# One hand-written issue order for the opening of layer 0, and four smaller moves

## The chip, the cores and the metric

The kernel runs on one core of one Trainium2 chip. The metric is the time of one execution on the device in microseconds (us), as the median of several runs. The core has five engines with a queue each: PE multiplies matrices (its weight loads are listed as PEld), DVE does vector work, ACT evaluates functions, POOL is a second, general engine for vector work, and SP issues the DMA transfers here. Each engine works through its own list of instructions in order, and semaphores make one wait for another.

## The reference

Two layers work on 512 latent tokens and 256 context tokens of width 1024. Cut to what the change touches:

```python
sc, scc = silu(c), silu(c_ctx)                  # the two conditions
for l in range(2):
    shift, scale, gate = split(sc @ w_mod[l] + b_mod[l])        # context: the same with scc
    hx = rms_norm(x, norm_w[l]) * (1 + scale) + shift           # hc: context, with its own shift and scale
    z  = hx @ w_in[l]                           # q, k, v of three attentions, LRU, gates, merges
    # three attentions (MLA, windowed SWA, dense AXA) and an RG-LRU, each times silu(gate),
    # projected and summed with sigmoid(merge) weights
    x  = x + gate * (mix @ w_out[l])            # context too, in layer 0 alone
# the RG-LRU uses softplus(-lambda), the same numbers for all tokens
```

## The kernel before, in words

Activations lie with channels on the 128 partitions. The width of 1024 is eight tiles `xk[k]`, each with 512 columns of latent and 256 of context. Products that need more than one pass of reduced precision are split: a number is a high part (fp32r, made by ACT) and a low part (the rest, made by a subtraction), and `mm3` (lines 193 to 197) multiplies high by high, low by high and high by low. So each weight slot passes DMA, ACT (`hi`) and POOL (`lo`, line 190) before PE can finish with it, and each `hx` tile passes ACT twice (lines 331, 332) and DVE once (line 333).

The opening of layer 0 (lines 893 to 970) does these things:

- `cond` (line 252, PE, and 254, ACT) spreads the two condition vectors over all partitions as rows `crow` in the buffer `P`. It is done three times: in the opening, again in the LRU stage of layer 0 and again late in layer 1, since `P` is used by attention in between.
- `sumsq`, `rstd_cols`, `rstd_rows` find 1/rms of each token: squares on ACT, sums over tiles on DVE (line 290), over partitions on PE (line 299), the power on POOL (line 304), and PE spreads it to `rb` in PSUM (line 310). `normal` (line 929) multiplies `xk` with it on DVE, for latent and context.
- `scale_pe` (line 227) makes the scales of two tiles on PE from 1 MB of `wmod0`, followed by two transposes (line 232) and two small DVE steps (lines 236, 238). `shift0` (line 243) makes the shift of one tile and one stream on DVE from a 128x1024 product; there are 16 of these.
- `hx_split` makes the high and low parts of `hx`, and `first` multiplies them with the weights of `sq` and `skv`, the projections of SWA, into six PSUM tiles `tk`: tiles t = 0 and 2 are latent, t = 4 is context.

After the opening come the head norms of these six products (`head_norm`, lines 384 to 410, with several steps on POOL each), the product of `akv` (`tg`, lines 195 to 197), two gates (`fg`), and then attention with projections beside it. `vectors` (lines 148 to 176) makes softplus by a chain of small DVE steps and a power on POOL.

The order in which instructions stand on each engine is set by the framework's scheduler, which plays the program through with its own estimates; `issue_after` binds one instruction behind another. The weights of the opening share a ring of two raw buffers (line 187) with all others.

Of the kernel before, what the change touches and what calls it, by code (L numbers as in the profile page):

```python
# [6 lines left out]
F32 = mybir.dt.float32  # L7
# [52 lines left out]
NS = len(SLOT)  # L60


def body(tc, xT, ccol, wmod, wmod0, pvec, rvec, tabs, wall, out):
# [5 lines left out]
    with st:  # L69
# [64 lines left out]
        xs = dp.tile([4, 128, 2, SEQ], F32, name="xs")  # L134

# [6 lines left out]
        def consts():  # L142
            sp.dma_start(out=tb, in_=tabs[:, :TB_N])
            mask = raw_take()[:, :256]
            sp.dma_start(out=mask, in_=tabs[:, TB_N:])
            dve.tensor_copy(out=maskb, in_=mask)

        def vectors():
# [72 lines left out]
        def scale_pe(c, scol, ws, p, pm):  # L221
# [9 lines left out]
            for e in range(2):  # L231
                last = pe.matmul(out=pm[:, 2 * e:2 * e + 2], lhsT=r[0:2, e * 128:e * 128 + 128], rhs=ident[0:2, 0:2],
                          start=True, stop=True, skip_group_check=True)
# [6 lines left out]
            return last  # L240
# [41 lines left out]
        def sumsq(xk, k, state, acc=None):  # L282
# [43 lines left out]
        def hx_split(k, i, h, xk):  # L326
# [6 lines left out]
            dve.tensor_tensor(out=h[:, 1, sl], in0=xk[:, sl], in1=h[:, 0, sl].bitcast(F32), op=ALU.subtract)  # L333
# [175 lines left out]
        pend = []  # L509

# [37 lines left out]
        def attn_tail(P, L, den, t0, nl, v, vh, done):  # L548
            dve.reciprocal(out=den, in_=den)
# [341 lines left out]

        scol = silu_col()
        xt = [big(f"x{kp}") for kp in range(4)]
        for kp in range(4):
            sp.dma_start(out=xt[kp][:, :, :SEQ], in_=xT[kp][:, :, :SEQ])
        wm = [mod0_load(0)]
        sp.dma_start(out=pv, in_=pvec)
        for kp in range(4):
            sp.dma_start(out=xt[kp][:, :, SEQ:], in_=xT[kp][:, :, SEQ:])
        xk = [xt[k // 2][:, k % 2, :] for k in range(KT)]  # L900
        sc = [cond(scol, i, crow[i]) for i in range(2)]
        states = [{}, {}]
# [4 lines left out]
        bank = lambda name: ps.tile([128, 512], F32, name=name, tag=name)  # L907
        rb, mp = bank("rb"), bank("mp")
        w0 = {'sq': [], 'skv': []}
# [3 lines left out]
        def wload0(key):  # L913
            hi, lo = [sb.tile([128, 512], F32R, name="w0", tag="w0", bufs=16) for i in range(2)]
            return wsplit(0, key, 512, hi, lo)

        def first(k, ts):
# [9 lines left out]
        def normal(i, k):  # L927
            o, n = SEGS[i]
            dve.tensor_tensor(out=xk[k][:, o:o + n], in0=xk[k][:, o:o + n], in1=rb[:, :n], op=ALU.mult)
# [5 lines left out]
        ms = rstd_cols(states[0], SEQ, mp[:, 384:])  # L935
        last = [scale_pe(0, scol, wm[0], mp, mp[:, 256:])]
        rstd_rows(ms, SEQ, rb)
        for c in range(4):
            for g in w0:
                w0[g].append(wload0((g, c)))  # L940
            if c < 3:
                wm.append(mod0_load(c + 1))
                with tc.issue_after(last[0].ins):
                    last[0] = scale_pe(c + 1, scol, wm[c + 1], mp, mp[:, 256:])
            ks = (2 * c, 2 * c + 1)
            for k in ks:
                shift(0, k)
            if c == 0:
                for k in range(KT):
                    normal(0, k)  # L950
            for k in ks:
                hx_split(k, 0, hx[k], xk[k])
                shift(1, k)
            for k in ks:
                first(k, (0, 2))
            if c == 0:
                for k in range(KT):
                    sumsq(xk[k][:, SEQ:], k, states[1], rawt[:, 1024:1280])
                with tc.issue_after(last[0].ins):
                    ms = rstd_cols(states[1], CTX, mp[:, 384:])  # L960
# [233 lines left out]
```

## Time and profile before

| | |
|---|---|
| median of 3 runs | 1438.25 us (1431.86 to 1442.55) |
| the profiled execution | 1437.18 us, of it 1435.1 us from its first to its last instruction |
| PE busy | 1357.7 us, 95% of the span |
| DVE, ACT, POOL busy | 895.2, 675.9 and 712.3 us |
| chain that ended last | PE 72%, DVE 9%, POOL 7%, DMA 5%, issue 4%, ACT 3% |
| mean granted clock of TensorE | 0.98 of full speed |

The opening is the first 90 us of the 1435. The page gives its busy time in slices of 36 us, which is too coarse, so the rows below are from views with smaller windows. In the view of stretches each row is a stretch of time; then comes its length, the busy time and instruction count of PE, PEld, DVE, ACT and POOL, the granted TensorE clock (1 is the full 2.4 GHz, 0.5 is 1.2 GHz), the DMA engines' busy share and GB/s. In the timeline each row gives the start, the busy time, the engine, the line of the kernel, the operation, what it writes and reads with shapes, and how many are merged; brackets hold the idle time before it and what ended it.

### The profile page before, as it was taken

The numbers are of one execution on the slowest core, as the hardware profiler recorded it, in microseconds if no ns is written. First come the engines' busy times: TensorE is split into PE (matmuls) and PEld (weight loads), VectorE is DVE, ScalarE is ACT, GpSimd is POOL, SyncE is SP. The second block draws the span as 40 slices with busy tenths as digits, with TensorE's granted clock in tenths as the row PEclk, the third lists the DMA queues.
The fourth block names the chain that finished last, engine by engine and source line by source line (L and its number), as shares of the span: only waits on it lengthen the run. The fifth ranks groups of instructions, "written<-read, shape, count | busy, mean of one in ns | idle before, by whom it ended". The sixth has DMA issues, their size and how long they took to land.

```text
span 1435.1 us, 21997 instructions
## 1 busy us (share of the span) xinstructions
PE 1357.7 (95%) x8216; PEld 1189.2 (83%) x8216; DVE 895.2 (62%) x1473; ACT 675.9 (47%) x1413; POOL 712.3 (50%) x691
## 2 busy tenths in 40 slices
PE   6898999999999999999999889999999999898998
PEld 4697989999998897888888778998887777776786
DVE  7756876456747656677445777876577576466441
ACT  4544555445544444562232344655555454465331
POOL 1453614223624625577553466455345563478663
PEclk8899999999999999999999999999999999999999
DMA  9301101111111212322335732112221111222544
GB/s 353 92 5 59 34 16 55 42 45 39 54 37 38 59 30 81 103 65 98 125 114 158 234 95 75 45 48 74 67 61 45 61 57 39 59 67 66 188 153 144
DMA packets 58746, 117.81 MB, mean 82 GB/s; under 512 B 6544, under 2 KB 10640, under 8 KB 58640
## 3 DMA queue, kind: packets, MB, share of 16 engines
q1 hardware_dynamic: 58640, 116.42, 25.7%
q8 instruction: 64, 1.05, 0.3%
q14 instruction: 42, 0.34, 0.1%
HBM read 112.20 MB, written 4.19 MB: 81 GB/s over the span
## 4 chain that ended last, share of the span: by engine, by line
PE 72%; DVE 9%; POOL 7%; DMA 5%; issue 4%; ACT 3%; SPq 0%; POOLq 0%; ACTq 0%; DVEq 0%
PE fg L196 9%; PE fg L195 9%; PE fg L197 9%; PE pvo L567 4%; DMA wraw<-in_wall_dram 3%; PE tg L197 3%; PE tg L196 3%; PE tg L195 3%; PE s L587 3%; POOL wlo L190 3%; PE pj L195 2%; PE pj L196 2%; PE pj L197 2%; PE ptr L560 2%; PE ptr L561 2%
## 5 line engine op out<-in xcount | busy, mean ns | idle before, releaser
L190 POOL TENSOR_TENSOR wlo<-wraw,whi 128x512 fp32r<-128x512 f32 (+2 forms) x290 | 398.8, 1378 | 360.9 <-ACT whi L189 347.3
L196 PE MATMUL fg<-hx,wlo 128*128 128x512 f32 (+1 forms) x864 | 314.2, 364 | 12.3 <-POOL wlo L190 12.3
L195 PE MATMUL fg<-hx,whi 128*128 128x512 f32 (+1 forms) x864 | 313.9, 365 | 7.9 <-ACT whi L189 5.0
L197 PE MATMUL fg<-hx,whi 128*128 128x512 f32 (+1 forms) x864 | 312.0, 361 | 0.0
L189 ACT ACTIVATE whi<-wraw 128x512 fp32r<-128x512 f32 (+2 forms) x290 | 179.8, 621 | 229.2 <-DMA wraw<-in_wall_dram 154.4
L196 PEld LDWEIGHTS fg<-hx,wlo 128*128 128x128 f32 x864 | 166.4, 193 | 38.9 <-POOL wlo L190 16.3
L195 PEld LDWEIGHTS fg<-hx,whi 128*128 128x128 f32 x864 | 165.6, 192 | 33.8 <-ACT whi L189 7.1
L197 PEld LDWEIGHTS fg<-hx,whi 128*128 128x128 f32 x864 | 166.1, 192 | 22.2
L564 DVE TENSOR_TENSOR PT<-ptr,PT 128x512 fp32r<-128x512 f32 (+1 forms) x148 | 98.5, 672 | 60.6 <-ACT PT L563 59.3
L196 PE MATMUL tg<-whi,hx 128*128 128x256 f32 (+1 forms) x432 | 122.5, 285 | 1.9 <-DVE hx L323 1.9
L195 PE MATMUL tg<-whi,hx 128*128 128x256 f32 (+1 forms) x432 | 122.2, 285 | 1.8 <-ACT hx L322 1.2
L197 PE MATMUL tg<-wlo,hx 128*128 128x256 f32 (+1 forms) x432 | 121.5, 284 | 1.4 <-POOL wlo L190 1.4
L563 ACT ACTIVATE PT<-ptr 128x512 fp32r<-128x512 f32 (+1 forms) x148 | 84.7, 585 | 79.6 <-PE ptr L561 70.0
L537 ACT ACTIVATE P<-s,nm 128x768 f32<-128x768 f32 (+3 forms) x120 | 91.9, 771 | 55.7 <-DVE nm L532 30.1
L530 DVE TENSOR_REDUCE nm<-s 128x2 f32<-128x1536 f32 (+3 forms) x60 | 86.0, 1434 | 29.5 <-PE s L197 16.9
L865 POOL TENSOR_TENSOR acc<-acc,gt 128x768 f32<-128x768 f32 (+1 forms) x48 | 81.1, 1690 | 24.1 <-DVE gt L861 23.2
L196 PEld LDWEIGHTS tg<-whi,hx 128*128 128x128 f32 x432 | 82.6, 191 | 2.8 <-DVE hx L323 2.5
L195 PEld LDWEIGHTS tg<-whi,hx 128*128 128x128 f32 x432 | 82.5, 191 | 2.8 <-ACT hx L322 1.4
L197 PEld LDWEIGHTS tg<-wlo,hx 128*128 128x128 f32 x432 | 82.4, 191 | 2.2 <-POOL wlo L190 2.0
L853 ACT ACTIVATE gt<-fg 128x512 f32<-128x512 f32 x84 | 44.1, 525 | 74.5 <-PE fg L197 70.9
L551 DVE TENSOR_SCALAR P<-P,den 128x768 f32<-128x768 f32 (+3 forms) x120 | 77.4, 685 | 1.8
L560 PE MATMUL ptr<-ident,P 128*128 128x128 f32 x288 | 72.9, 279 | 1.9 <-DVE gt L861 1.8
(302 smaller groups left out, 3137.2 us busy)
## 6 DMA issues: line engine op xcount, KB each, us to landing
wraw<-in_wall_dram SPq DMA_DIRECT2D x286, 256.0 KB, 2.6
raw<-in_wmod_dram SPq DMA_DIRECT2D x32, 512.0 KB, 3.6
wmp<-in_wmod_dram SPq DMA_DIRECT2D x16, 512.0 KB, 8.6
x<-in_xT_dram SPq DMA_DIRECT2D x4, 512.0 KB, 5.7
xs<-xn SPq DMA_DIRECT2D x4, 512.0 KB, 3.9
gt<-xs SPq DMA_DIRECT2D x8, 256.0 KB, 2.9
out_dram<-xn SPq DMA_DIRECT2D x4, 512.0 KB, 3.8
wraw<-in_wall_dram SPq DMA_DIRECT2D x8, 160.0 KB, 2.2
```

Of the source, the lines that this page charges most:

```text
L189: act.activation(out=hi[:, :n], in_=raw, func=AF.Copy)
L190: pool.tensor_tensor(out=lo[:, :n], in0=raw, in1=hi[:, :n].bitcast(F32), op=ALU.subtract)
L195: pe.matmul(out=o, lhsT=a[0], rhs=b[0], start=first, stop=False, skip_group_check=True)
L196: pe.matmul(out=o, lhsT=a[1], rhs=b[0], start=False, stop=False, skip_group_check=True)
L197: pe.matmul(out=o, lhsT=a[0], rhs=b[1], start=False, stop=last, skip_group_check=True)
L530: dve.tensor_reduce(out=nm, in_=s3, axis=AX.X, op=ALU.max, negate=True)
L537: act.activation(out=P[i][:, :L], in_=s3[:, i, :], func=AF.Exp, scale=scale, bias=nm[:, i:i + 1], accum_out=den[:, i:i + 1])
L551: dve.tensor_scalar(out=P[i][:, :L], in0=P[i][:, :L], scalar1=den[:, i:i + 1], scalar2=None, op0=ALU.mult)
L560: pe.transpose(tr[:, e * 256:e * 256 + 128], P[0][:, ca:ca + 128], ident)
L563: act.activation(out=q[:, :n], in_=tr[:, :n], func=AF.Copy)
L564: dve.tensor_tensor(out=q[:, 512:512 + n], in0=tr[:, :n], in1=q[:, :n].bitcast(F32), op=ALU.subtract)
L865: pool.tensor_tensor(out=a[:, :N], in0=a[:, :N], in1=t[:, :N], op=ALU.add)
```

## The change

A wrapper `InOrder` binds every instruction that goes through it behind the one before it on its engine. The opening is written out in full with all five engines wrapped, so its order no longer comes from the scheduler. The new order is one list: which product comes when is written by hand, context's products of tiles 0 and 1 stand ahead of the latent products of tiles 4 and 5, and the load of `akv` (with its two subtractions per pair on POOL) closes the list. Besides:

- Two times 20 products of a bf16 identity with itself stand on PE before and after the opening's `cond`.
- For context, the sums of squares (line 290 before), the multiplication with 1/rms (line 929 before) and the low part of `hx` (line 333 before) go from DVE to POOL; the row of 1/rms is first copied from PSUM to SBUF by ACT (`rbc`), and POOL reads that.
- The eight weights of the opening have a ring of four raw buffers of their own.
- `vectors` runs later: its DVE steps are chained behind a reciprocal of an attention, where before they lay from 16 us on.
- The condition rows are written to DRAM (`cs`) once and read back by DMA in layers 0 and 1 where `cond` was repeated.

```diff
+class InOrder:
+    def __init__(self, tc, eng, last=None):
+        self.tc, self.eng, self.last = tc, eng, last
+    def __getattr__(self, name):
+        f = getattr(self.eng, name)
+        def call(*a, **k):
+            if self.last is None:
+                self.last = f(*a, **k)
+            else:
+                with self.tc.issue_after(self.last.ins):
+                    self.last = f(*a, **k)
+            return self.last
+        return call
...
-        def vectors():
+        def vectors(last):
+            dve = InOrder(tc, nc.vector, last)
...
-                dve.tensor_tensor(out=state['acc'][:, :n], in0=state['acc'][:, :n], in1=sq[:, :n], op=ALU.add)
+                eng = pool if acc is not None else dve
+                eng.tensor_tensor(out=state['acc'][:, :n], in0=state['acc'][:, :n], in1=sq[:, :n], op=ALU.add)
...
-            dve.tensor_tensor(out=h[:, 1, sl], in0=xk[:, sl], in1=h[:, 0, sl].bitcast(F32), op=ALU.subtract)
+            (pool if i else dve).tensor_tensor(out=h[:, 1, sl], in0=xk[:, sl], in1=h[:, 0, sl].bitcast(F32), op=ALU.subtract)
...
+        pe, act, dve, pool, sp = (InOrder(tc, e) for e in (nc.tensor, nc.scalar, nc.vector, nc.gpsimd, nc.sync))
...
+        def warm(n):
+            for i in range(n):
+                pe.matmul(out=mp[:, 384:512], lhsT=identb, rhs=identb, start=True, stop=True, skip_group_check=True)
...
+        warm(20)
         sc = [cond(scol, i, crow[i]) for i in range(2)]
+        warm(20)
...
+        rstd_rows(ms, CTX, rb)
+        act.activation(out=rbc, in_=rb[:, :CTX], func=AF.Copy)
+        for k in range(KT):
+            pool.tensor_tensor(out=xk[k][:, SEQ:], in0=xk[k][:, SEQ:], in1=rbc, op=ALU.mult)
+        w0_split(r0[2])
+        first(2)
+        turn()
+        scale_add(2, col(2))
+        first(3)
+        for k in (4, 5):
+            shift(0, k)
+        for k in (4, 5):
+            latent(k)
+        for k in (2, 3):
+            shift(1, k)
+        turn = scale_pe(3, scol, wm[3], mp, col(3))
+        for k in (0, 1):
+            context(k)
+        w0_split(r0[3])
+        for k in (0, 1):
+            first(k, (4,))
+        turn()
+        scale_add(3, col(3))
+        for k in (4, 5):
+            first(k)
...
+        akv = tload(0, 'akv')
+        boot = dve.last
+        pe, act, dve, pool, sp = nc.tensor, nc.scalar, nc.vector, nc.gpsimd, nc.sync
         consts()
+        for i in range(2):
+            sp.dma_start(out=cs[i], in_=sc[i])
...
             if l == 0:
-                with tc.issue_after(wdma[0].ins):
-                    vectors()
+                vectors(mark[0])
...
             if l == 0:
-                sc = [cond(scol, i, crow[i]) for i in range(2)]
+                for i in range(2):
+                    sp.dma_start(out=sc[i], in_=cs[i])
...
             if l == 1:
-                sc = [cond(scol, 0, crow[0])]
+                sp.dma_start(out=sc[0], in_=cs[0])
```

How the change moves instructions is shown at three places. In these rows `w_` are weights, with an even and odd number for high and low parts, `xms` is 1/rms, `wmp_0` to `wmp_3` the four 512 KB pieces of a group of modulation weights, and a line of "..." stands for rows left out. In the new program nearly all rows have the line of the wrapper, 76.

POOL in the opening, before:

```order
L304 TENSOR_TENSOR xms<-xms,mhalf 128x4
L190 TENSOR_TENSOR w_216<-wraw,w_215 128x512
L190 TENSOR_TENSOR w_222<-wraw,w_221 128x512
L190 TENSOR_TENSOR w_337<-wraw,w_336 128x512
L190 TENSOR_TENSOR w_343<-wraw,w_342 128x512
L190 TENSOR_TENSOR w_460<-wraw,w_459 128x512
L304 TENSOR_TENSOR xms<-xms,mhalf 128x2
```

POOL in the opening, now:

```order
L76 TENSOR_TENSOR raw<-raw,gt 128x256 x7
L76 TENSOR_TENSOR w_381<-w0r,w_380 128x512
L76 TENSOR_TENSOR w_385<-w0r,w_384 128x512
L76 TENSOR_TENSOR xms<-xms,mhalf 128x2
L76 TENSOR_TENSOR x_118<-x_118,raw 128x256 x2
L76 TENSOR_TENSOR x_119<-x_119,raw 128x256 x2
L76 TENSOR_TENSOR x_120<-x_120,raw 128x256 x2
L76 TENSOR_TENSOR x_121<-x_121,raw 128x256 x2
L76 TENSOR_TENSOR w_440<-w0r,w_439 128x512
L76 TENSOR_TENSOR w_444<-w0r,w_443 128x512
L76 TENSOR_TENSOR hx_0_242<-x_118,hx_0_242 128x256
L76 TENSOR_TENSOR hx_1_243<-x_118,hx_1_243 128x256
```

Seven sums, eight multiplications and eight low parts of context (six of these come later) now stand between the subtractions of the weights.

PE around the last group of scales, before (`tk_189` and `tk_190` are the two products of context):

```order
L232 MATMUL mp<-ident,raw 128x2 x2
L195 MATMUL tk_189<-w_215,hx_0_175 128x256
L195 MATMUL tk_190<-w_221,hx_0_175 128x256
L227 MATMUL mp<-wmp_0_471,scol 2x256 x4
L227 MATMUL mp<-wmp_1_472,scol 2x256 x4
L196 MATMUL tk_189<-w_215,hx_0_175 128x256
```

PE at the same place, now (`tk_254` and `tk_255` are the products of context):

```order
L76 MATMUL mp<-wmp_0_407,scol 2x256 x4
L76 MATMUL mp<-wmp_1_408,scol 2x256 x4
L76 MATMUL tk_254<-w_276,hx_0_242 128x256 x2
L76 MATMUL tk_254<-w_277,hx_0_242 128x256
...
L76 MATMUL mp<-ident,raw 128x2 x2
L76 MATMUL tk<-w_439,hx_4_246 128x256 x2
```

Between the two parts of the last piece stand the rest of context's products of tiles 0 and 1; the latent products of tiles 4 and 5 stand behind them.

SP's transfers up to the second group of scale weights, before:

```order
L218 DMA wmp_2_125<-in_wmod_dram 128x1024
L897 DMA consts<-in_pvec_dram 128x114
L218 DMA wmp_3_126<-in_wmod_dram 128x1024
L899 DMA x_115<-in_xT_dram 128x2x256
L899 DMA x_116<-in_xT_dram 128x2x256
L216 DMA wmp_0_227<-in_wmod_dram 128x1024
L188 DMA wraw<-in_wall_dram 128x512
L216 DMA wmp_1_228<-in_wmod_dram 128x1024
L218 DMA wmp_2_229<-in_wmod_dram 128x1024
L188 DMA wraw<-in_wall_dram 128x512
```

SP's transfers up to the same weights, now:

```order
L76 DMA wmp_3_129<-in_wmod_dram 128x1024
L76 DMA consts<-in_pvec_dram 128x114
L76 DMA w0r<-in_wall_dram 128x512 x2
L76 DMA x_118<-in_xT_dram 128x2x256
L76 DMA x_119<-in_xT_dram 128x2x256
L76 DMA x_120<-in_xT_dram 128x2x256
L76 DMA x_121<-in_xT_dram 128x2x256
L76 DMA wmp_0_143<-in_wmod_dram 128x1024
L76 DMA wmp_1_144<-in_wmod_dram 128x1024
```

All of context and the first two weights now stand ahead of the second group of scale weights.

## Rows read from the trace of the kernel before

**Rows 1.** The page's first line: length of the profiled execution

```profile
span 1435.1 us, 21997 instructions
```

**Rows 2.** Stretches: length, busy PE, PEld, DVE, ACT, POOL, clock, DMA share, GB/s

```profile
0.00:15.00 15.00, 8.56 (x40) 8.31 (x40) 5.40 (x13) 8.11 (x15) 0.68 (x6) 0.93 0.82 288
15.00:31.10 16.10, 12.56 (x44) 4.84 (x44) 15.96 (x34) 5.95 (x13) 5.11 (x3) 0.75 1.04 398
31.10:65.00 33.90, 26.61 (x148) 18.78 (x147) 29.44 (x73) 16.83 (x29) 14.17 (x10) 0.85 0.40 135
65.00:88.70 23.70, 23.70 (x195) 23.40 (x195) 8.85 (x19) 11.62 (x24) 5.44 (x6) 1.00 0.13 34
88.70:106.30 17.60, 17.60 (x148) 17.46 (x146) 14.42 (x35) 6.68 (x20) 16.50 (x21) 1.00 0.01 2
106.30:124.10 17.80, 12.60 (x72) 10.21 (x71) 12.33 (x23) 7.72 (x20) 12.58 (x14) 0.94 0.28 86
...
200.00:250.00 50.00, 50.00 (x368) 46.89 (x368) 32.95 (x69) 28.52 (x77) 17.06 (x28) 1.00 0.14 43
```

**Rows 3.** Timeline of PE: start, busy time, engine, line, operation, idle before

```profile
3.31 6.69 PE L252 MATMUL scb<-ident,scol 128*128 128x128 f32 x32 [3.31 <-DVE scol L209]
...
25.90 5.30 PE L227 MATMUL mp<-wmp,scol 128*2 128x256 f32 x16 [3.29 <-DVE mod L236]
...
31.80 0.60 PE L232 MATMUL mp<-ident,raw 2*128 2x2 f32 x4
...
50.20 3.62 PE L227 MATMUL mp<-wmp,scol 128*2 128x256 f32 x16
...
108.02 0.50 PE L196 MATMUL fg<-hx,wlo 128*128 128x512 f32 x1 [1.55 <-POOL wlo L190]
```

**Rows 4.** Timeline of ACT in the opening and at its end

```profile
22.74 0.63 ACT L189 ACTIVATE w<-wraw 128x512 fp32r<-128x512 f32 x1 [1.33 <-DMA wraw<-in_wall_dram]
...
83.96 0.60 ACT L491 ACTIVATE raw<-tk 128x512 f32<-128x512 f32 x1 [5.11 <-PE tk L197]
```

**Rows 5.** Timeline of POOL where DVE works beside it

```profile
20.20 1.77 POOL L190 TENSOR_TENSOR w<-wraw,w 128x512 fp32r<-128x512 f32 x1 [2.85 <-ACT w L189]
23.45 1.27 POOL L190 TENSOR_TENSOR w<-wraw,w 128x512 fp32r<-128x512 f32 x1 [1.47 <-ACT w L189]
42.41 4.00 POOL L190 TENSOR_TENSOR w<-wraw,w 128x512 fp32r<-128x512 f32 x2 [17.69 <-ACT w L189]
```

**Rows 6.** Timeline of DVE at the same times, and a step of softplus

```profile
20.77 2.01 DVE L290 TENSOR_TENSOR raw<-raw,gt 128x256 f32<-128x256 f32 x2
22.70 3.07 DVE L929 TENSOR_TENSOR x<-x,rb 128x512 f32<-128x512 f32 x5
...
41.77 1.28 DVE L243 CUSTOM_DVE_ANT_0 raw<-wmp,P,consts 128x1024 bf16<-128x1024 f32 x1
...
42.97 2.30 DVE L243 CUSTOM_DVE_ANT_0 wmp<-wmp,P,consts 128x1024 f32<-128x1024 f32 x1
...
45.21 1.75 DVE L333 TENSOR_TENSOR hx<-x,hx 128x512 fp32r<-128x512 f32 x1
...
54.69 0.17 DVE L163 TENSOR_TENSOR sp_ab<-sp_ab,sp_u 128x8 f32<-128x8 f32 x1
```

**Rows 7.** Timeline of POOL: small powers, the head norms' begin, a gate's weight

```profile
49.47 0.70 POOL L304 TENSOR_TENSOR xms<-xms,mhalf 128x2 f32<-128x2 f32 x1
50.14 1.63 POOL L156 TENSOR_TENSOR sp_u<-ebase,sp_ab 128x8 f32<-128x8 f32 x1
...
86.03 0.57 POOL L373 TENSOR_SCALAR hn_ss<-hn_ss 128x8 f32<-128x8 f32 x1 [16.05 <-DVE hn_ss L393]
...
106.65 1.32 POOL L190 TENSOR_TENSOR wlo<-wraw,whi 128x512 fp32r<-128x512 f32 x1
```

**Rows 8.** Timeline of POOL in the MLA stage: a step with 256 columns

```profile
539.85 0.73 POOL L682 TENSOR_TENSOR y<-y,pvt 64x256 f32<-64x256 f32 x1 [2.65 <-DVE pvt L681]
```

**Rows 9.** Chain of waits, layers 0 and 1: start (us), duration (us), what

```profile
544.26 0.89 PE scb L252 x8
...
1327.14 2.70 DMA wraw<-in_wall_dram
```

More of the change, by code (lines that the diff above doesn't have):

```diff
@@ L230, in scale_pe, with scale_add @@
             act.activation(out=r[0:2, :256], in_=p[0:2, :256], func=AF.Copy)
-            for e in range(2):
-                last = pe.matmul(out=pm[:, 2 * e:2 * e + 2], lhsT=r[0:2, e * 128:e * 128 + 128], rhs=ident[0:2, 0:2],
-                          start=True, stop=True, skip_group_check=True)
+            return lambda: [pe.matmul(out=pm[:, 2 * e:2 * e + 2], lhsT=r[0:2, e * 128:e * 128 + 128], rhs=ident[0:2, 0:2],
+                                      start=True, stop=True, skip_group_check=True) for e in range(2)]
+        def scale_add(c, pm):
             f = 8 + 2 * c
@@ L509, in body @@
         pend = []
+        mark = [None]
         def attn_flush():
@@ L548, in attn_tail @@
         def attn_tail(P, L, den, t0, nl, v, vh, done):
-            dve.reciprocal(out=den, in_=den)
+            mark[0] = dve.reciprocal(out=den, in_=den)
             for i in range(2):
@@ L933, in shift @@
             shift0(k, i, sc[i], w, w if i else rawt[:, 1536:2048].bitcast(BF16))
-        ms = rstd_cols(states[0], SEQ, mp[:, 384:])
-        last = [scale_pe(0, scol, wm[0], mp, mp[:, 256:])]
-        rstd_rows(ms, SEQ, rb)
[L938 to L960, printed above, removed]
-                last[0] = states[1]['ins']
-                rstd_rows(ms, CTX, rb)
-            for k in ks if c else ():
-                normal(1, k - 2)
-                hx_split(k - 2, 1, hx[k - 2], xk[k - 2])
-                first(k - 2, (4,))
@@ L967, in body, with latent, context @@
-        for k in (6, 7):
-            normal(1, k)
-            hx_split(k, 1, hx[k], xk[k])
-            first(k, (4,))
+        def latent(k):
+            hx_split(k, 0, hx[k], xk[k])
+        rbc = rawt[:, 1280:1536]
+        def context(k):
+            hx_split(k, 1, hx[k], xk[k])
+        col = lambda c: mp[:, 260 + 4 * c:264 + 4 * c]
+        turn = scale_pe(0, scol, wm[0], mp, col(0))
+        ms = rstd_cols(states[0], SEQ, mp[:, 288:])
+        turn()
+        scale_add(0, col(0))
+        w0_split(r0[0])
@@ new lines, in body @@
+        for k in (0, 1):
+            shift(0, k)
+        rstd_rows(ms, SEQ, rb)
+        for k in (0, 1):
+            normal(k)
+        for k in (0, 1):
+            latent(k)
+        turn = scale_pe(1, scol, wm[1], mp, col(1))
+        for k in range(2, KT):
+            normal(k)
+        first(0)
+        turn()
+        scale_add(1, col(1))
+        first(1)
+        for k in range(KT):
+            sumsq(xk[k][:, SEQ:], k, states[1], rawt[:, 1024:1280])
+        w0_split(r0[1])
+        r0.append(w0_load(2))
@@ new lines, in body @@
+        ms = rstd_cols(states[1], CTX, mp[:, 288:])
+        for k in (2, 3):
+            shift(0, k)
+        for k in (2, 3):
+            latent(k)
+        for k in (0, 1):
+            shift(1, k)
+        wm.append(mod0_load(3))
+        r0.append(w0_load(3))
+        turn = scale_pe(2, scol, wm[2], mp, col(2))
+        rstd_rows(ms, CTX, rb)
+        act.activation(out=rbc, in_=rb[:, :CTX], func=AF.Copy)
+        for k in range(KT):
+            pool.tensor_tensor(out=xk[k][:, SEQ:], in0=xk[k][:, SEQ:], in1=rbc, op=ALU.mult)
@@ new lines, in body @@
+        for k in (6, 7):
+            shift(0, k)
+        for k in (6, 7):
+            latent(k)
+        for k in (2, 3):
+            context(k)
+            first(k, (4,))
+        for k in (6, 7):
+            first(k)
+        for k in (4, 5, 6, 7):
+            shift(1, k)
+        for k in (4, 5, 6, 7):
+            context(k)
+            first(k, (4,))
+        akv = tload(0, 'akv')
+        boot = dve.last
+        pe, act, dve, pool, sp = nc.tensor, nc.scalar, nc.vector, nc.gpsimd, nc.sync
```

50 lines of the change are left out of this document (36 added, 14 removed).

## The prediction

> **What bounds the kernel now.** The kernel as a whole is bound by PE. But the opening, where the change lies, is bound by something else in each stretch, so I read the view of stretches first [rows 2]. From 0 to 15 us the data arrive; from 15 to 31.1 DVE is busy 15.96 of 16.1 us while PE has 12.56 at a granted clock of 0.75; from 31.1 to 65 PE works 26.61 of 33.9 and DVE 29.44; from 65 on PE works without a gap. So about 3.5 + 7.3 = 10.8 us of PE idle time lie between 15 and 65, and only they can be won, together with the clock. The end of this stage is not PE alone: the products `tk` end at 88.7, and POOL starts on the head norms at 86.03, 16.05 us after its last work [rows 7], 2.1 us after ACT emptied the first `tk` at 83.96 [rows 4]. From there POOL is busy 16.50 of 17.6 us [rows 2], and the gate's `wlo` comes at 106.65 at the end of POOL's chain [rows 7]; PE waited 1.55 us for it and goes on at 108.02 [rows 3]. What the opening gives is therefore what POOL's start moves, as long as PE's own `akv` is not later.
>
> The timeline of PE says what an idle time costs twice: 3.29 us of idle before 25.90, and then the scales of two tiles in 5.30 us, which take 3.62 at 50.20 [rows 3]. The timelines of POOL and DVE side by side [rows 5, 6] show a second matter. A subtraction of 128x512 on POOL takes 1.27 us at 23.45, though DVE multiplies with PSUM beside it in its usual 3.07/5 = 0.61. But at 20.20 it takes 1.77, while two DVE additions of SBUF with SBUF take 2.01; at 42.41 two take 4.00, while DVE's shift takes 2.30 for 1.28 and its subtraction 1.75. Steps that read two SBUF operands on both engines go one after the other here.
>
> This rests on rows alone. The Trainium skill, page "SBUF — State Buffer", section "Who interferes with whom", says the same: the ports that the two engines share are an exclusive lock, which a DVE step with two SBUF inputs contends for with a POOL step that reads SBUF, and a DVE step with one such input does not; the rows agree. It speaks against moving work to POOL here. Against it stands its page "Perfetto Trace Analysis", section "Optimizing Scalar/DVE Operations", by which moving work from a saturated vector engine may make sense, with a warning of that port: by the first, all 23 moved steps cost DVE time; by the second they cost none and the first rival's time results.
>
> **The new opening, worked as a list.** Prices from rows: a matmul of `tk` 23.70/195 = 0.12 us [rows 2], so 24 for a latent tile 2.9 and 12 for a context tile 1.45; scales 3.6, two transposes and any spread 0.6 [rows 3]; POOL 1.3 for 128x512, 0.70 for a small power [rows 7], and 0.73 for 256 columns (the nearest row has 64 partitions, [rows 8]; between 0.6, half of 1.27, and 1.0); DVE 1.28 for a shift and 0.6 for a subtraction [rows 5, 6].
>
> The 40 added products of the identity stand where PE has nothing else: the first twenty before `scol` (PE waited 3.31 us for it, [rows 3]), the others between `cond`'s end at 10.0 and the first weights. At the 0.12 us of a `tk` product twenty take 2.4 us; cost 0, at most 1 us if the weights come early.
>
> *Start.* The second piece of the second group of scale weights now has as many bytes ahead of it as the second `wraw` had, which ACT got at 22.74 [rows 4]. So PE begins those scales at 22.7 (25.90 before) and ends at 26.3; latent tile 0, transposes, latent tile 1: 32.7. Context's squares stand on ACT behind the copy of those scales, so POOL's seven sums run from 27.4 for 5.1 us, to 32.5: level with PE. Then 0.5 on PE (33.2), two `wlo` with one DVE shift between them 2.6 + 1.2 and the power 0.7 (about 37.8), the spread 0.6 (38.4), and ACT's copy behind tile 3's parts: 39.5.
>
> *The middle.* From 39.5 POOL has eight multiplications (5.8), two `wlo` (2.6) and context's first low part (0.7); DVE has six shifts (7.7) and two subtractions (1.2) that take turns with them: 18.0 us, to about **57.3**. PE meanwhile: scales 36.8, spread and a wait 38, latent 2, transposes, latent 3 and the last scales 3.6 + small waits: 48.8. The next instruction on PE is context's product of tile 0, which needs that low part; the latent products of tiles 4 and 5, whose data are there, stand behind it. So a hole of 8.3 us opens at 48.8. Behind it are eight context tiles (11.7), four latent (11.7) and transposes (0.6), 24 us with about 1 us of waits for later low parts: 82.3. The clock after the hole: 3.29 idle cost 5.30 - 3.62 = 1.7 us, taken as 1.5. `tk` ends at **83.8** (88.7 before).
>
> *What comes of it.* The first four products are now finished four context tiles, 5.8 us, before that end, 4.7 before (88.7 - 83.96); POOL's head norms start at 83.8 - 5.8 + 2.1 = 80.1, 5.9 us earlier. But two subtractions of `akv` now stand on POOL ahead of the norms or beside them, +2.6 in that chain at most. The gate comes **3.5 us earlier**; PE's own chain (83.8 + 17.6 = 101.4) is before it and doesn't bind. Bounds: 0 (the hole larger by 4) to the first rival's 14.5.
>
> **The other edits.** *Condition rows.* In layer 0 `cond`'s matmuls lie on the chain in four pieces of 0.89 us from 544.26 on [rows 9], and PE is full there: at most -3.6. In their place SP reads 1 MB; at 398 GB/s [rows 2] that is 2.6 us. It stands in SP's queue, and a weight behind it is late if `P` is not yet free; the DMA at 34 to 43 GB/s in such stretches [rows 2] has room. I take -3.0 (0 to -3.6). In layer 1 the chain runs through a DMA at 1327.14 [rows 9] and not through `cond`: two pieces, -0.4 (0 to -1.8). The write of `cs` goes when DMA runs at 2 GB/s [rows 2]: 0. *Softplus.* Some 30 DVE steps of 0.17 to 0.2 us [rows 6], 6 us with gaps, and a POOL power of 1.63 [rows 7] move into attention behind a reciprocal. At 200 to 250 us PE is busy 50.00 of 50 and DVE 32.95 [rows 2]: it covers most of it; +1 (0 to +6, all of it in front of a DVE step that PE waits for). *The rest of layer 0* is laid out anew by the scheduler around other starting times: 0, with +/-4 as the size of the pieces above, since no row shows it.
>
> **Sum:** -3.5 - 3.0 - 0.4 + 1 = -5.9. The profiled execution took 1437.2, of it a span of 1435.1 [rows 1], so 1431.3; the median of the runs is 1 us above this execution, less than they differ among themselves, so I leave it at **1431**. One per cent is 14.4 us, about what a measurement of this kernel can tell from no change.
>
> **Rivals.** *First: the ports don't bind, PE does.* If POOL's work on context runs beside DVE without taking turns, the first low part is there before 48.8 and PE has no hole: 48.8 + 24 = 72.8 for the end of `tk`, POOL starts at 69.1, 16.9 earlier, less 2.6: the gate 14.3 to 14.5 earlier. With -2.4 from the rest: -17, **1420**. For it: the `wlo` at 23.45 had its full speed beside DVE [rows 5], and more of DVE's steps than I count could fall into PE's own waits. Against it: 20.20 and 42.41. Half of the hole gives 1425. Together 0.25.
>
> *Second: the opening gives nothing.* The sums come later than 32.5, or the 128-partition step on POOL takes 1.0 instead of 0.73 (8 x 0.3 = 2.4, and as much for the sums), or the change does not do what it says: the added products stand before 13 us and fill neither the hole at 48.8 nor the one at 21, where the clock falls just as before. Then `tk` ends at 87 to 88 and the added `wlo` take the rest: 1437.2 - 2.4 = **1435** to 1438. Chance 0.14.
>
> *Third, slower: the hole keeps the clock low.* Of 65 to 88.7 PE ran at 1.00, since nothing stopped it; from 15 to 31.1 it had 0.75, half of the time at 1.2 GHz, from holes of 3.3 us [rows 2, 3]. If after 8 us of idle, and with further short waits for context's low parts, the clock stays at 1.2 GHz to the end of `tk`, the 25 us behind the hole become 50: `tk` ends at 107, `akv` at 107 + 17.6 = 125 against 106.3 before, +18 to the gate, and with -2.4 from the rest about **1453**. It is slower than before from about 9 us of work at the low clock on, since `tk` then ends after 88.7 by more than the 2.4 won elsewhere, and by over 1% from about 23. For it: the clock was 0.85 from 31.1 to 65, where PE has only short waits [rows 2]. Against it: at 50.20 the scales are back at 3.62 us [rows 3]. Chance 0.06.
>
> **Numbers.** Forecast 0.55, rivals 0.25, 0.14, 0.06. The unknown rest (+/-4) and softplus (+6) widen the forecast to 1426 to 1438. The range goes from 1419, the whole of the first rival without the last us, to 1441, the second with softplus uncovered; the third stays out. Faster by over 1% (below 1423.9) takes most of the first rival and a tail of the forecast: 0.25. Slower by over 1% is the third and a share of badly placed softplus and rest: 0.08. Within 1%: 0.67.
>
> **What would show it.** The low part of context's tile 0 on POOL at about 57, and PE idle before it from about 49: right for the middle; a PE without a gap from 33 to 73 is the first rival. POOL's multiplications of 256 columns at a mean near 1.5 instead of 0.73, and shifts over 1.28, show the turns. The end of `tk` at 84 and the gate's `wlo` at 103 give the opening; the second `cond` missing between 544 and 550 and no new wait of PE for a DMA there give the 3.0; no DVE wait of PE where softplus lies gives the 1. Wrong it would be made by a hole that PE does not have, by a clock that stays at 0.5, or by a scheduler that puts the softplus steps in front of an attention step on the chain.

## The result and the profile after

The changed kernel takes **1445.5 us** (median of 14 runs, 1439.6 to 1449.1) where the kernel before takes 1438.3: a ratio of 1.0053, 95% interval 1.0038 to 1.0067. The forecast was 1431, the range 1419 to 1441. It is 7 us slower and not 6 faster. The profiled execution took 1443.6, of it

```profile
span 1441.8 us, 22007 instructions
```

against 1435.1 [rows 1]. The stretches of [rows 2] in the changed kernel, with the same columns:

```profile
0.00:15.00 15.00, 10.46 (x80) 8.21 (x81) 5.25 (x13) 8.68 (x15) 0.68 (x6) 0.89 0.81 281
15.00:31.10 16.10, 13.64 (x76) 8.35 (x75) 9.81 (x18) 7.26 (x15) 7.93 (x7) 0.89 1.05 395
31.10:65.00 33.90, 26.80 (x176) 21.21 (x176) 22.69 (x33) 15.18 (x26) 26.45 (x21) 0.90 0.40 156
65.00:88.70 23.70, 22.17 (x183) 21.77 (x183) 15.64 (x29) 16.09 (x34) 19.40 (x18) 1.00 0.20 56
88.70:106.30 17.60, 15.73 (x112) 14.70 (x112) 14.53 (x32) 5.68 (x17) 16.57 (x21) 0.93 0.05 16
106.30:124.10 17.80, 15.07 (x80) 12.60 (x79) 12.37 (x25) 8.19 (x20) 8.37 (x8) 0.88 0.28 74
```

Up to 31 us DVE is freed (9.81 for 15.96 us busy) and PE's clock is better (0.89 for 0.75); from 31 to 65 POOL has nearly doubled (26.45 for 14.17). Behind the opening PE, full before from 88.7 to 106.3, has gaps, and its clock is 0.88 from 106.3 to 124.1. PE's timeline of the opening (start, busy time, ..., idle before):

```profile
22.33 5.00 PE L76 MATMUL mp<-wmp,scol 128*2 128x256 f32 x16 [1.15 <-DMA wmp<-in_wmod_dram]
...
46.32 3.62 PE L76 MATMUL mp<-wmp,scol 128*2 128x256 f32 x16
50.94 0.39 PE L76 MATMUL tk<-w,hx 128*128 128x256 f32 x1 [1.01 <-ACT hx L76]
56.43 4.26 PE L76 MATMUL tk<-w,hx 128*128 128x256 f32 x23 [5.10 <-POOL hx L76]
...
68.77 14.75 PE L76 MATMUL tk<-w,hx 128*128 128x256 f32 x119 [1.53 <-POOL hx L76]
83.36 0.28 PE L216 MATMUL tg<-whi,hx 128*128 128x256 f32 x1
```

The wait for context's first low part is there, 5.1 us where 8.3 were forecast, and `tk` ends at 83.4, forecast 83.8. Kernels below whose opening is the same have this end between 83.4 and 86.0 in their one profile each, so a difference of 2 us there says little. POOL and DVE beside it:

```profile
40.89 9.94 POOL L76 TENSOR_TENSOR x<-x,raw 128x256 f32<-128x256 f32 x8 [1.74 <-ACT raw L76]
54.67 2.39 POOL L76 TENSOR_TENSOR hx<-x,hx 128x256 fp32r<-128x256 f32 x2
...
75.22 2.56 POOL L76 TENSOR_TENSOR wlo<-wraw,whi 128x512 fp32r<-128x512 f32 x2
77.87 0.20 POOL L395 TENSOR_SCALAR hn_ss<-hn_ss 128x8 f32<-128x8 f32 x1
80.15 1.29 POOL L76 TENSOR_TENSOR wlo<-wraw,whi 128x512 fp32r<-128x512 f32 x1
82.90 1.58 POOL L76 TENSOR_TENSOR wlo<-wraw,whi 128x512 fp32r<-128x512 f32 x1
101.58 1.26 POOL L211 TENSOR_TENSOR wlo<-wraw,whi 128x512 fp32r<-128x512 f32 x1
```

```profile
42.65 1.73 DVE L76 CUSTOM_DVE_ANT_0 wmp<-wmp,P,consts 128x1024 f32<-128x1024 f32 x1
51.31 2.28 DVE L76 CUSTOM_DVE_ANT_0 wmp<-wmp,P,consts 128x1024 f32<-128x1024 f32 x1
```

Eight multiplications take 9.94 us, 1.24 each, where the first of them takes 0.74 ([rows 8] has 0.73 on 64 partitions), and shifts take 1.6 to 2.3 for 1.28: the two engines take turns. The head norms start at 77.87 (86.03 before), but *four* `wlo` of `akv` stand in and ahead of them. PE then waits for POOL's chain and for the first keys:

```profile
102.90 0.50 PE L217 MATMUL fg<-hx,wlo 128*128 128x512 f32 x1 [1.87 <-POOL wlo L211]
116.89 0.39 PE L610 MATMUL s<-kT0sq,qT0sq 128*128 128x256 f32 x1 [2.67 <-ACT kT0sq L484]
```

The kernel before has the same two waits, 1.55 us before 108.02 [rows 3] and this one:

```profile
121.60 0.39 PE L587 MATMUL s<-kT0sq,qT0sq 128*128 128x256 f32 x1 [2.92 <-ACT kT0sq L462]
```

So the gaps are not new, they come 5 us earlier, and at the first score of SWA 4.7 us are in hand. To see where they are lost, compare the times at which both kernels have multiplied the same number of columns on PE (without the products of `cond` and of the identity, 2,697,808 in each). By this count the changed kernel is 5.1 us ahead at 165 us of the kernel before, 1.1 at 195, 0.2 at 400; it is 1.6 behind at 450, 1.3 at 527, 3.3 at 671, 4.5 at 1150, 7.1 at 1170 and 6.1 at the end. Two of these losses are looked at here. In the last attention pairs of SWA (165 to 195 us) PE has 24.61 us of 30 at a clock of 0.89, and at 535 to 570, where `cond` is gone, 27.01 of 35 at 0.87; the changed kernel, then the kernel before:

```profile
165.00:195.00 30.00, 24.61 (x145) 20.92 (x145) 19.87 (x46) 15.88 (x46) 5.26 (x15) 0.89 0.03 11
535.00:570.00 35.00, 27.01 (x151) 22.93 (x149) 21.21 (x39) 12.95 (x28) 13.81 (x12) 0.87 0.23 74
```

```profile
165.00:195.00 30.00, 26.65 (x165) 22.79 (x164) 21.50 (x50) 17.53 (x51) 7.97 (x19) 0.94 0.06 18
535.00:570.00 35.00, 31.47 (x198) 27.99 (x198) 22.78 (x40) 15.66 (x31) 17.92 (x14) 0.95 0.22 76
```

The 2.6 us from 1150 to 1170 come behind three waits (0.59, 1.78 and 0.47 us) that the kernel before has too (0.59, 1.76 and 0.48); behind them the clock is 0.83 here (1160 to 1175) and 1.00 there, and in a_nosp, a kernel below with the same waits, it is 1.00 and nothing is lost. The change rewrites no step that stands there, and what decides it was not looked for.

At 535 to 570 PE waits twice for DVE's normalization of the last attention tails, and DVE for POOL; first PE, then DVE, then POOL:

```profile
549.08 0.33 PE L583 MATMUL ptr<-ident,P 128*128 128x128 f32 x1 [2.63 <-DVE P L574]
550.89 0.47 PE L584 MATMUL ptr<-ident,P 128*128 128x128 f32 x1 [1.48 <-DVE P L574]
```

```profile
547.19 3.64 DVE L574 TENSOR_SCALAR P<-P,den 128x256 f32<-128x256 f32 x2
```

```profile
547.08 1.80 POOL L787 TENSOR_TENSOR lx<-lx,lx 128x768 fp32r<-128x768 f32 x1 [4.90 <-ACT lx L786]
548.83 1.85 POOL L888 TENSOR_TENSOR acc<-acc,gt 128x768 f32<-128x768 f32 x1
```

The same two steps in the kernel before, 1.4 us ahead of POOL's, and PE in the same stretch:

```profile
545.49 0.62 DVE L551 TENSOR_SCALAR P<-P,den 128x256 f32<-128x256 f32 x2
```

```profile
544.10 1.05 PE L252 MATMUL scb<-ident,scol 128*128 128x128 f32 x8
546.49 1.06 PE L252 MATMUL scb<-ident,scol 128*128 128x128 f32 x8
547.82 1.06 PE L252 MATMUL scb<-ident,scol 128*128 128x128 f32 x8
548.83 1.05 PE L252 MATMUL scb<-ident,scol 128*128 128x128 f32 x8
```

Two steps in 0.62 us there, 3.64 beside POOL here; and `cond`'s products, which the forecast took for work on the path, filled PE's time beside these tails.

### The profile page after: what moved, and what is told of

It is laid out like the page before. It is cut to its first block, busy times and chain, and to the rows that moved or that the text cites. A ratio compares the mean times of both kernels' runs of the same rounds, so it can differ in the third digit from the quotient of the medians.

```text
span 1441.8 us, 22007 instructions
## 1 busy us (share of the span) xinstructions
PE 1358.3 (94%) x8208; PEld 1189.1 (82%) x8208; DVE 903.4 (63%) x1450; ACT 674.1 (47%) x1408; POOL 741.3 (51%) x714
## 5 line engine op out<-in xcount | busy, mean ns | idle before, releaser
L574 DVE TENSOR_SCALAR P<-P,den 128x768 f32<-128x768 f32 (+3 forms) x120 | 82.5, 728 | 1.7
L583 PE MATMUL ptr<-ident,P 128*128 128x128 f32 x288 | 73.6, 282 | 5.5 <-DVE P L574 2.9
L584 PE MATMUL ptr<-ident,P 128*128 128x128 f32 x288 | 72.6, 282 | 2.4 <-DVE P L574 2.3
```

Source lines behind the costliest of these rows:

```text
L574: dve.tensor_scalar(out=P[i][:, :L], in0=P[i][:, :L], scalar1=den[:, i:i + 1], scalar2=None, op0=ALU.mult)
L583: pe.transpose(tr[:, e * 256:e * 256 + 128], P[0][:, ca:ca + 128], ident)
```

## The experiments

Each kernel was timed with the kernel before beside it. Theory 1: what the change moved or took away had covered a wait. Theory 2: the scheduler's new order behind the opening costs the time, whatever the edits. "Length of the LRU stage" is the time on PE from the first `lz` product to the 85th `pj` product behind it, which the expectations call the 89th (141.6 us before, 143.7 after).

**Softplus.** a_sp binds it as before the change, a_nosp leaves its series out (two of its results are other numbers).

```diff
-                vectors(mark[0])
+                with tc.issue_after(wdma[0].ins):
+                    vectors()
```

> The changed kernel with softplus bound as before the change (behind a weight's transfer, not behind a reciprocal of attention), so its thirty DVE steps lie in the opening. Theory 1 (what the change took away or moved had covered something): softplus in attention costs the 4.1 us by which PE's products drift from -1.4 us at 206 to +2.75 at 260, so 1445.5 - 4 = 1441.5, less what the steps cost in the opening (0 to 2). Theory 2 (the scheduler's new order of the rest of layer 0 costs the time, whatever the edits): within 1 us of 1445.5, since the order behind the opening hardly changes here.

> The changed kernel without softplus's series and its power (two short DVE steps fill its two result tiles with other numbers), the rest in nearly the same order. This sizes softplus in attention: the forecast's +1 gives 1444.5, its upper bound of 6 gives 1439.5; if attention hides all of it, 1445.5.

a_sp: 1447.4, ratio 1.0070 (1.0051 to 1.0089). a_nosp: 1445.7, 1.0060 (1.0039 to 1.0080). Without it nothing is won, so in attention softplus costs nothing that shows; in the opening `tk` ends at 88.1, and the whole is 1.8 us slower by the medians, which the intervals do not tell from nothing. Theory 1 fails for softplus: that move is harmless.

**The products of the identity.** a_nowarm takes out both `warm(20)`.

> The changed kernel without the two times 20 products of the identity. The order behind them stays as it is but for a few neighbours. Forecast's step: 0, since the scales wait for their weights at 12.03 us in any case; cond takes 6.7 instead of 4.3 us and ends at 10. If the products hold the clock up for the scales at 12 us, those take 5.0 without them as with them (they take 5.03 now), so 1445.5 +/- 1. A rival: a lower clock in the first scales makes the opening 1 to 2 us later, 1447.

1445.8, 1.0055 (1.0033 to 1.0077): nothing, as forecast.

**The middle of the opening.** a_fill moves PE's latent products into the wait; a_nrm takes the multiplications off POOL.

```diff
+        for k in (4, 5):
+            first(k)
         for k in (0, 1):
             first(k, (4,))
         turn()
         scale_add(3, col(3))
-        for k in (4, 5):
-            first(k)
```

```diff
-        act.activation(out=rbc, in_=rb[:, :CTX], func=AF.Copy)
         for k in range(KT):
-            pool.tensor_tensor(out=xk[k][:, SEQ:], in0=xk[k][:, SEQ:], in1=rbc, op=ALU.mult)
+            dve.tensor_tensor(out=xk[k][:, SEQ:], in0=xk[k][:, SEQ:], in1=rb[:, :CTX], op=ALU.mult)
```

> The changed kernel with the latent products of tiles 4 and 5 moved on PE ahead of context's products of tiles 0 and 1, into the wait of 5.10 us at 51. If that wait is only a matter of PE's order, 5.8 us of products fill it, tk ends 4 to 5 us earlier (about 79 us), the clock does not drop, and the gate comes 2 to 4 us earlier: 1442. If POOL's chain sets the gate, tk ends earlier but the gate does not: 1445.5. The scheduler lays the rest of layer 0 out anew here, worth +/-3 by itself.

> The changed kernel with context's eight multiplications by 1/rms back on DVE, from PSUM (0.33 us each), and without the copy of the row; sums and low parts stay on POOL, and the order behind the opening is almost the same. If POOL and DVE take turns at SBUF, POOL's first low part of context comes 5 us or more earlier than 54.67 (eight steps at a mean of 1.4 fall out of its list), PE's wait of 5.10 us at 51 shrinks to under 1.5, tk ends near 80 and the gate 2 to 4 us earlier: 1442 to 1443.5. If the turns cost nothing there, POOL saves 5.8 us of its own all the same, but DVE's shifts stay at 1.7 to 2.3 us beside the remaining steps and the wait shrinks by the same; told apart by the mean of the shifts.

a_fill: 1440.5, 1.0020 (1.0003 to 1.0038). But not by what was expected of it. PE's timeline shows the wait only moved, behind the later scales:

```profile
52.67 1.65 PE L76 MATMUL tk<-w,hx 128*128 128x256 f32 x6 [2.19 <-POOL w L76]
...
70.79 0.58 PE L76 MATMUL tk<-w,hx 128*128 128x256 f32 x1 [5.52 <-ACT hx L76]
```

and `tk` ends at 88.7. What it has is another order of attention: from 165 to 195 PE is busy 26.76 us at 0.94, as in the kernel before, and by the count of columns it loses nothing there (3.7 us ahead at 165, 4.0 at 195). a_nrm: 1441.1, 1.0028 (1.0011 to 1.0044). The first low part comes at 54.38, no earlier, as it now waits for ACT; PE's waits there fall from 6.1 to 3.2 us, with a new one of 0.82 before the last scales:

```profile
53.72 0.39 PE L76 MATMUL tk<-w,hx 128*128 128x256 f32 x1 [1.79 <-ACT hx L76]
55.53 4.33 PE L76 MATMUL tk<-w,hx 128*128 128x256 f32 x23 [1.42 <-POOL hx L76]
```

```profile
45.46 2.73 DVE L76 TENSOR_TENSOR x<-x,rb 128x256 f32<-128x256 f32 x8
48.38 1.28 DVE L76 CUSTOM_DVE_ANT_0 raw<-wmp,P,consts 128x1024 bf16<-128x1024 f32 x1
```

DVE makes the eight in 2.73 us, and the two shifts behind them are back at 1.28 each: the turns were what the multiplications cost. `tk` ends only 0.9 earlier, so most of the 4.4 us by the medians is not located in this one profile.

**The condition rows.** a_cond makes them on PE again in both layers, a_cond0 in layer 0 alone; a_dummy reads them back *and* makes the 32 products for nobody.

```diff
-                for i in range(2):
-                    sp.dma_start(out=sc[i], in_=cs[i])
+                sc = [cond(scol, i, crow[i]) for i in range(2)]
```

> The changed kernel with the condition rows made again on PE in both layers, nothing written to or read from DRAM. Theory 1: the 32 products on PE in layer 0 filled PE's wait for the last attention tails; with them back the waits of 2.63 and 1.48 us near 550 and the half clock behind them vanish, PE's products drift +1.5 instead of +5 at 560, and the time is 2 to 4 us below 1445.5. Theory 2: no change, 1445.5 +/- 1. The forecast's own step (PE time saved) says 3 us slower than the changed kernel, 1449.

> The changed kernel with cond kept on PE in layer 0 alone; layer 1 reads its row back. Layer 0's stage as with cond kept in both (141.8 instead of 143.7), and layer 1 as in the changed kernel. The forecast's -0.4 (0 to -1.8) for layer 1 then gives 1443.2 - 0.4 = 1442.8; if layer 1's products were a cover too, it is 1443.2 + 1 or more.

> The changed kernel, rows still read back from DRAM in layer 0, and the 32 products of cond made besides on PE, their output used by nobody. If cond's products were only a cover for PE's wait behind the attention tails (and kept its clock), these do the same: from PE's first lz product to its 89th pj product the kernel before took 141.6 us, the changed one 143.7, with cond kept 141.8; expected here 142 +/- 0.7, and 1443 to 1444 in all. If instead the reading back (1 MB ahead of weights in SP's queue) makes the loss, it stays at 143.7 or more, and 1445 to 1449 in all.

a_cond 1443.2, 1.0040 (1.0024 to 1.0057), LRU stage 141.8; a_cond0 1441.6, 1.0027 (1.0012 to 1.0042), stage 139.5. So in layer 0 the rows in DRAM *cost* 3.9 us (a_cond0). a_dummy: stage 142.1 as expected, but 1445.6 in all, 1.0064 (1.0042 to 1.0086): PE's waits for DVE's normalization fall from 4.1 to 1.0 us, and nothing is won in the whole, against 3.9 us in a_cond0 (the two intervals just touch). Why was not found, and in this order of the program the reading back is not cleared.

**akv and its order.** a_akv takes one call out of the hand-written list.

```diff
-        akv = tload(0, 'akv')
         boot = dve.last
         pe, act, dve, pool, sp = nc.tensor, nc.scalar, nc.vector, nc.gpsimd, nc.sync
+        akv = tload(0, 'akv')
         consts()
```

> The changed kernel with one thing taken out of the hand-written order: the load of akv with its subtractions is left to the scheduler, as before. The opening's list is otherwise the same, and softplus and the rows in DRAM stay. By its order PE has 30 + 14 products of a gate beside the last two latent attention pairs of SWA again, as in the kernel before, where the changed kernel has 26 + 11. Theory 2 (the scheduler's order costs time by itself): from PE's first gate product to the 73rd score of SWA the kernel before took 108.2 us, the changed one 111.3 with 5.4 us of PE idle between 165 and 195; here 108 or less with 3.4 us, and 1442 +/- 1 in all. If the order is no cause, 1445.5.

> The changed kernel with akv left to the scheduler and cond kept on PE in layer 0: the hand-written opening without its two side effects. If the two causes add, 1445.5 - 3.9 (cond in layer 0) - 3.5 (order of attention) = 1438; the forecast's own terms for what is left (opening -3.5, layer 1 -0.4, softplus +1) say 1435.5. If they don't add, 1441.

a_akv: **1438.0**, 1.0012 (0.9998 to 1.0027), 7.5 us less by one line. a_akv_c0: 1434.0, 0.9976 (0.9962 to 0.9989), another 4.0, so the two causes add. In a_akv's opening the scheduler puts two of `akv`'s `wlo` between context's sums on POOL and the other two ahead of context's first low part; PE waits longer, and `tk` ends at 89.4; yet behind it:

```profile
83.40:125.00 41.60, 40.07 (x290) 37.34 (x289) 32.09 (x72) 17.36 (x48) 32.19 (x36) 1.00 0.13 39
165.00:195.00 30.00, 26.50 (x176) 22.81 (x175) 21.55 (x46) 17.79 (x52) 6.98 (x16) 0.94 0.08 21
```

PE is busy 40.07 of 41.6 us at full clock where the changed kernel has

```profile
83.40:125.00 41.60, 37.00 (x238) 33.35 (x238) 30.24 (x62) 15.79 (x42) 28.69 (x33) 0.92 0.16 47
```

with POOL's `wlo` among the head norms, and the gap at 165 to 195 has closed as far as in the kernel before. PE's order shows why there: beside the last two latent pairs 30 and 14 products of a gate stand in the kernel before and in a_akv, 26 and 11 in the changed one, which has used the others up. All profiles of this record agree: the nine kernels with 26 and 11 lose 3.4 to 4.2 us against the kernel before between 165 and 195 by the count of columns, and the seven others with 30 and 14 (a_fill, whose list ends with `akv`, is one of them) lose at most 0.2. By the same count a_akv is 4.9 us ahead at 165, 4.8 at 195 and 4.0 at 450, the changed kernel 5.1 and 1.1 ahead and then 1.6 behind. So the four `wlo` at the end of the list cost nothing up to 165 against the four in the opening; the loss comes behind it, with the order of attention, though no kernel changed that order alone. The 73rd score of SWA starts at 209.5 in a_akv, 211.97 in the changed kernel and 214.27 before.

**Cover or transfer; layer 1.** k_dummy and k_cond both have `akv` left to the scheduler; k_dummy also makes `cond`'s products for nobody, and k_cond keeps `cond` in both layers.

```diff
                 for i in range(2):
+                    for e in range(2):
+                        p = gps("scb")
+                        for k in range(4):
+                            c = 2 * (4 * e + k) + i
+                            pe.matmul(out=p[:, k * 128:k * 128 + 128], lhsT=scol[:, c:c + 1].to_broadcast([128, 128]),
+                                      rhs=ident, start=True, stop=True, skip_group_check=True)
                     sp.dma_start(out=sc[i], in_=cs[i])
```

> The changed kernel with akv left to the scheduler (1438.0), rows still read back in layer 0, and the 32 products of cond made besides, for nobody. If cond's products were a cover on PE, this comes near the kernel that keeps cond (1434.0): 1434 to 1436, and PE's waits for DVE's normalization near 550 are under 1.5 us in all. If the 1 MB read back makes the loss, it stays at 1438 or goes up by the 3.6 us of the products, to 1441.

> The changed kernel with akv left to the scheduler and cond kept on PE in both layers, no rows in DRAM. It differs from the one at 1434.0 in layer 1 alone. The forecast's layer 1 term says 1434.0 + 0.4 (0 to +1.8); if layer 1's products are a cover as in layer 0, it is 1432 to 1434; if they stand on PE's path there, 1436 to 1438.

k_dummy: **1431.0**, 0.9961 (0.9946 to 0.9977). 32 products whose output nobody reads make the kernel 7.0 us *faster* than a_akv, and no slower than a_akv_c0 (1434.0), which reads nothing back in layer 0: in this order the transfer costs nothing that shows. The view of PE's waits from 526 to 560 us, a_akv and then k_dummy (total, times, longest):

```profile
PE fg L216 <- ACT whi L210: 2.2, 1, 2.2
PE ptr L584 <- DVE P L574: 1.6, 1, 1.6
PE pvo L590 <- DVE PT L587: 1.4, 1, 1.4
PE ptr L583 <- DVE P L574: 1.2, 1, 1.2
PE fg L217 <- POOL wlo L211: 0.3, 1, 0.3
```

```profile
PE fg L216 <- ACT whi L210: 2.0, 1, 2.0
PE pvo L590 <- DVE PT L587: 1.4, 1, 1.4
PE fg L217 <- POOL wlo L211: 0.7, 1, 0.7
```

Both waits for DVE's normalization are gone. PE has products to run meanwhile, and DVE's two steps take 0.62 us at 540.54, ahead of POOL's `lx` at 541.98, where in a_akv they took 2.46: with other work on PE the scheduler has set two other steps of DVE (`pvt` and `gt`), which stand ahead of them in a_akv, behind them. So cover and order changed together, and neither was tried by itself. In a_cond0 and in a_dummy DVE's steps still take 1.8 to 1.9 each beside POOL's and only the cover is new: PE waits 0.88 + 1.48 us in the one, which is 3.9 us faster, and 1.0 in the other, which is no faster. The stage is 137.1 us long, 144.7 in a_akv and 139.9 with `cond` itself. k_cond: 1436.8, 1.0011 (0.9991 to 1.0031), 2.8 us over a_akv_c0: in layer 1 the reading back *is* a gain. k_cond's `tk` ends late, as in all four kernels with this opening and `akv` left to the scheduler (89.0 to 91.3):

```profile
89.01 0.28 PE L216 MATMUL tg<-whi,hx 128*128 128x256 f32 x1
```

**A better opening.** n_open reorders the middle; best adds akv left to the scheduler and `cond` in layer 0, best_dummy also k_dummy's products in `cond`'s place.

```diff
-        act.activation(out=rbc, in_=rb[:, :CTX], func=AF.Copy)
         for k in range(KT):
-            pool.tensor_tensor(out=xk[k][:, SEQ:], in0=xk[k][:, SEQ:], in1=rbc, op=ALU.mult)
+            dve.tensor_tensor(out=xk[k][:, SEQ:], in0=xk[k][:, SEQ:], in1=rb[:, :CTX], op=ALU.mult)
         w0_split(r0[2])
+        for k in (0, 1):
+            context(k)
         first(2)
...
-        for k in (2, 3):
-            shift(1, k)
         turn = scale_pe(3, scol, wm[3], mp, col(3))
-        for k in (0, 1):
-            context(k)
-        w0_split(r0[3])
         for k in (0, 1):
             first(k, (4,))
         turn()
         scale_add(3, col(3))
-        for k in (4, 5):
-            first(k)
+        w0_split(r0[3])
         for k in (6, 7):
             shift(0, k)
         for k in (6, 7):
             latent(k)
+        for k in (4, 5):
+            first(k)
+        for k in (2, 3):
+            shift(1, k)
...
```

> The changed kernel with the middle of the opening in another order: context's multiplications on DVE from PSUM, context's tiles 0 and 1 split ahead of latent 4 and 5, the last transposes and scales ahead of the latent products of tiles 4 and 5. PE's waits of 1.0 and 5.1 us near 50 vanish, tk ends at 76 +/- 1.5 instead of 83.4, and POOL's head norms start near 71. Against 1445.5: -4.4 as with the multiplications alone, and another 3 to 5 if PE's order made the rest of the wait: 1437 to 1439. If attention behind it can't use an earlier start, 1441.

> All of it together: the other order of the opening's middle with context's multiplications on DVE, akv left to the scheduler, cond kept on PE in layer 0, the row read back in layer 1. If the effects add: 1445.5 - 3.9 - 3.5 - 7 = 1431, faster than both kernels. If the gates or attention take back half of the opening's gain, 1434 to 1436.

> The version at 1426.6 (other order of the opening's middle, akv left to the scheduler, cond kept on PE in layer 0) with the rows read back in layer 0 and the 32 products made for nobody in cond's place. The same edit took 1434.0 to 1431.0 (3 us), and 1438.0 to 1431.0 against the read back alone: if the cover adds to the opening's gain, 1423 to 1425; if the order of the stage differs so that the waits come back, 1427 to 1431.

n_open: 1442.3, 1.0029 (1.0013 to 1.0046): the opening is faster (the first gate product comes 96.2 us after the start, 100.6 in the changed kernel), and most of it is given back, as the last sentence of its expectation said: PE waits 3.08 and 5.65 us on the way to the first score of SWA, which starts at 118.88, later than the changed kernel's. With `akv` free it counts. best: 1426.6, 0.9930 (0.9907 to 0.9953), 7.4 us below a_akv_c0, from which it differs in the middle of the opening alone; **best_dummy: 1420.7, 0.9883** (0.9864 to 0.9903), faster than both kernels. In best's opening (31.1 to 65 and 65 to 88.7 us) PE is busy 52 of 57.6 us at full clock:

```profile
31.10:65.00 33.90, 29.05 (x203) 23.23 (x203) 24.98 (x39) 17.89 (x31) 23.04 (x18) 1.00 0.51 193
65.00:88.70 23.70, 23.16 (x192) 22.92 (x192) 20.65 (x38) 12.00 (x29) 17.26 (x19) 1.00 0.00 1
```

## Why the prediction was wrong, point by point

- **The opening: right in its steps; what it is worth at the end stays open.** `tk`'s end (83.4 for 83.8) and the gate's `wlo` (101.58 for 103) came as forecast, and 5.1 us are in hand at 165 for the 3.5; the turns of POOL and DVE are there, and a_nrm removed them with the multiplications. The hole is 3.2 us shorter, as PE came to it 2.5 us later (51.3 for 48.8), and it ends when the low part is there, 56.4 for 57.3, so `tk`'s end does not hang on its length. Two of the sums slip by 0.2 (39.5 + 18.0 is 57.5, 57.3 - 48.8 is 8.5), which changes nothing. k_cond, the hand-written opening without the rows in DRAM and without `akv` in the list, is 1.0011 of the kernel before (0.9991 to 1.0031), no gain that can be measured. But its `tk` ends at 89.0, as `akv`'s subtractions stand inside its opening; in its profile, the fastest of its 12 executions, it is 5.2 us ahead at 165 and still 5.1 at 671. No run has the early end of `tk` without `akv` in the list, and best, whose PE is busy 52 us of 57.6 in the opening where the changed kernel has 49, did gain 7.4 by its middle.
- **The step that failed by most: "*The rest of layer 0* is laid out anew by the scheduler around other starting times: 0, with +/-4".** Closing the list with `akv` costs 7.5 us by the medians (a_akv), 5.9 by the ratios to the kernel before. POOL's chain is not the reason: four subtractions stand in it, and not the two that the forecast priced at 2.6, but the gate came earlier than forecast, and at 165 us the changed kernel and a_akv are equally far ahead (5.1 and 4.9). What the kernels that lose have in common is the order of attention: the scheduler spends the gate's products before the attention pairs that need them, and 4.0 us go between 165 and 195, where a_akv loses 0.1; another 1.8 go between 400 and 450, where a_akv loses nothing. At the first product of the LRU stage a_akv is 5.5 ahead (522.3 for 527.8). What is left of the 7.5 is open; a_akv's profile is of the slowest of its 12 executions.
- **Condition rows in layer 0, "-3.0 (0 to -3.6)": wrong in sign.** Taking it back gained 3.9 and 4.0: +4, 7 us off. [Rows 9] are on the chain of waits, but in front of another chain, DVE's normalization, that ended barely earlier. Without the products PE waits for it (2.63 and 1.48 us) at a lower clock (0.87 for 0.95 from 535 to 570), and DVE's steps fall beside POOL's and take 3.64 us for 0.62; how much of the 4 us is the missing cover and how much DVE's order was not separated. On this the Trainium skill, page "SBUF — State Buffer", section "Who interferes with whom", names what the forecast left out: a `tensor_scalar` can run in a mode that uses both ports and then contends with POOL too. The trace agrees: one tensor operand, and yet 1.8 us a step, the length of POOL's.
- **Layer 1, "-0.4 (0 to -1.8)": right in sign, too small.** 2.8 us between k_cond and a_akv_c0; the 1.6 between a_cond and a_cond0 is inside their intervals.
- **Softplus, "+1 (0 to +6)": 0** (a_nosp +0.2). **The identity's products: 0**, as said.
- The third rival's sign was right, its mechanism was not: the clock was 0.62 from 57 to 60, some 3 us behind the hole's end, and then 1.00 (0.90 from 31.1 to 65, 1.00 from 65 to 88.7). That the kernel came out slower, as this rival alone had it, is luck.

## What to carry to other kernels

A piece on the chain of waits is worth its length only if no other chain ends close behind it; ask what the engine would wait for next, and what keeps its clock if the piece goes. Giving a scheduler other starting times is a change of its own, and can cost more than the edit: try the edit with the later order held as it was, one call at a time. And the end of one engine's stage is not the gain: `tk` ends 6 us later in a_akv than in the changed kernel, and both are equally ahead at 125 us (4.8 and 5.0). Two kernels whose orders differ are compared best at the same amount of work done, and several executions are needed, since one profile can lie some us from the median.

## What the runs showed of the hardware

Products for nobody can pay: in k_dummy 32 of them, some 4.2 us of PE's time in four pieces of 0.83 to 1.28, made the kernel 7.0 us faster, with another order of DVE's steps beside them. In a_dummy the same 32 gave nothing (1445.6 for 1445.5), and so did forty before the first weights (a_nowarm). A DVE step with a single tensor operand in SBUF (`P` times a column, 128x256) takes 0.31 us alone and 1.8 beside a POOL step with two. And the clock of PE is not settled by its waits alone: behind the same three waits near 1155 us (the longest 1.78) the changed kernel's execution ran at 0.83 for 15 us, and a_nosp's at 1.00.
